# The gate stage of a PEER layer written in one fixed order, with its u products cut in pieces between the groups

## The chip, the cores and the metric

The kernel runs on one core of a Trainium2 chip. The metric is the device time of one execution in microseconds, lower is better. Engines are named as in the profile: PE (TensorE; PEld is its weight load), DVE (VectorE), ACT (ScalarE), POOL (GpSimd) and SP (SyncE, which issues DMAs).

## The reference

Two transformer blocks on 512 tokens of 1024 features: a mixer with a mixture of experts, then a second block that ends in a PEER layer. The change lies in that last layer alone. Per token it scores two sets of 128 keys for each of 8 heads, takes the best 16 of each, the best 16 of their sums, and mixes 8 x 16 of 16,384 experts:

```python
q = (ht @ wq).reshape(t, PEER_HEADS, 2, PEER_DK)
...
va, ia = lax.top_k(sa, PEER_TOPK)
vb, ib = lax.top_k(sb, PEER_TOPK)
cand = va[..., :, None] + vb[..., None, :]
cidx = ia[..., :, None] * PEER_NKEYS + ib[..., None, :]
top, pos = lax.top_k(cand, PEER_TOPK)
eidx = jnp.take_along_axis(cidx, pos, axis=-1)
g = jax.nn.softmax(top, axis=-1)
a = jax.nn.gelu(jnp.einsum('thkd,td->thk', u_tab[eidx], ht))
return jnp.einsum('thk,thkd->td', g * a, v_tab[eidx])
```

## The kernel before

The 512 tokens are four tiles of 128. For the first three (ND = 384) the kernel does not gather experts: it computes the product of all 16,384 rows of u with the tokens, 128 rows at a time (the 128 "u products", L1607 to L1620), multiplies by a gate that is zero for experts that a token did not choose, and multiplies by the rows of v (`peer_v`, matmuls into `pacc`). The fourth tile gathers its rows (`Gather`). Rows are split in two f16 halves: uTh (high) by ACT, uTl (the rest) by DVE, or, with early=True, ACT scales the raw row in place as well (uTr) and POOL subtracts (`peer_parts`, L1597). A u product is 8 slices of three matmuls, 128x384 each (`mm3`): two with uTh, the third with uTl. ACT then applies gelu into `pa`.

The pacc loop needs u products well ahead of their use (LAG = 34), so class `Ahead` makes the first ones in earlier stages: `load` fetches and splits a row block, `multiply` runs the matmuls, `finish` runs gelu; calling the object does all three, `load` only where no block is ready.

The layer runs in stages. `peer_scores` (L1412) goes in 19 steps over 16 half heads (N = 16): query products `pq`, scores `ps`, `top16` on DVE (five passes: max, index, replace, max, index), and, one head later, `pairs` (candidate sums `cand` and numbers `cidx`), `pick_best` (best 16 of 50 and a mask `pickm`), `pick_which` and `pick_sum` (the chosen experts, `pef`). The last head's picks for three tiles come in steps 16 to 18, on DVE. Each of steps 9 to 18 makes one early u product, loading the next one first. `late` keeps the fourth tile's candidates for the pacc loop.

The gate stage (`peer_gates`, L1548) then goes over the three tiles. Per tile: softmax of the picks (`pgate`, with an exp on ACT, whose table is not that of gelu, so each change loads one), expert numbers cut in two digits (`gab`), three transposes on PE (`gtp`), copies to f16 (`gidx`, `gsp`). Then groups of GN = 16 tokens: four one-hot passes on DVE (`gob`, `goa`, `goh`, `goa`, 128x2048 each), 32 matmuls (`gg`), four copies by ACT into `gst`, and for each second group a DMA of 2 MB to `gates` in memory. There are 8 groups a tile, 24 in all. Some groups also call `Ahead`, up to 31 products (LAG - REST). The stage has no manual schedule here: the recording layer's scheduler sets the order of its instructions on each engine. Three products more (`rest`) and the pacc loop follow, in manual schedule.

Of the kernel before, what the change touches and what calls it, by code (L numbers as in the profile page):

```python
# [10 lines left out]
F32 = mybir.dt.float32  # L11
F16 = mybir.dt.float16
# [7 lines left out]
P = 128  # L20
# [3 lines left out]
D = 1024  # L24
# [11 lines left out]
GC = 32  # L36
GN = 16
GS = 10
LAG = 34
# [15 lines left out]
class Block:  # L55
# [1257 lines left out]
    def peer(self):  # L1313
# [5 lines left out]
        with ExitStack() as es:  # L1319
# [92 lines left out]
    def peer_scores(self, qp, vp, hl, top, ef, late, ahead):  # L1412
# [25 lines left out]
        with tc.manual_schedule(engines={ET.Pool, ET.PE, ET.DVE, ET.Activation}):  # L1438
# [3 lines left out]
            evacuate(0)  # L1442
            for n in range(N + 3):
                h, s = divmod(n, 2)
# [21 lines left out]
                if n > 1 and s == 0 and n <= N:  # L1466
                    cand[h - 1] = self.pairs(vp, qp, [val.pop(n - 2), val.pop(n - 1)], [idx.pop(n - 2), idx.pop(n - 1)], eng)
                    for tt, m in enumerate(self.pick_best(qp, [(cand[h - 1][0][:, tt], top[:, tt, h - 1]) for tt in range(3)], eng)):
                        picks[h - 1, tt] = m

                if n > 2 and s == 1:
                    for tt in range(ND // P):
                        self.pick_which(picks[h - 1, tt], cand[h - 1][1][:, tt], n < N)
                    for j in range(2):
                        nc.scalar.activation(late[j][:, h - 1], cand[h - 1][j][:, 3], AF.Copy)
                if s == 0 or n > 8:
                    ahead.finish()
                evacuate(n + 1)
                if n < N:
                    val[n] = vp.tile([P, 4, 16], F32, name="tv", tag="tv", bufs=4)  # L1480
                    idx[n] = vp.tile([P, 4, 16], F32, name="ti", tag="ti", bufs=4)
                    for tt in range(4):
                        iu[n, tt] = qp.tile([P, 16], U32, name="tiu", tag="tiu", bufs=8)
                    self.top16(qp, [(val[n][:, tt], iu[n, tt], ps[:, P * tt:P * (tt + 1)]) for tt in range(4)], P)

    def pairs(self, vp, qp, val, idx, eng):
# [14 lines left out]

    def pick_best(self, wk, xs, eng):

        nc = self.nc
        ps = [wk.tile([P, 16], U32, name="ppos", tag="ppos", bufs=3) for _ in xs]
        self.top16(wk, [(top, pos, cand) for pos, (cand, top) in zip(ps, xs)], 50)
        ms = []
        for pos in ps:
            posf = wk.tile([P, 16], F32, name="pposf", tag="pposf", bufs=3)
            eng.tensor_copy(posf, pos)  # L1510
            m = wk.tile([P, 8 * 20 + 8 * 50], F32, name="pickm", tag="pickm", bufs=5)
            for x, k, n in self.pick_parts(m):
# [34 lines left out]

    def peer_gates(self, wk, e, g, gd, tt, ahead):  # L1548

        nc = self.nc  # L1550
        f = wk.tile([P, 2, P], F32, name="gab", tag="gab", bufs=1)
        nc.vector.tensor_scalar(f[:, 0], e, 1.0 / 128, -63.5 / 128, op0=OP.mult, op1=OP.add)
        nc.vector.tensor_scalar(f[:, 0], f[:, 0], 1.5 * 2.0 ** 23, -1.5 * 2.0 ** 23, op0=OP.add, op1=OP.add)
        nc.vector.scalar_tensor_tensor(f[:, 1], f[:, 0], -128.0, e, op0=OP.mult, op1=OP.add)
        ps = self.ps1("gtp")
        for j, x in enumerate((f[:, 0], f[:, 1], g)):
            nc.tensor.transpose(ps[:, P * j:P * (j + 1)], x, self.ident)

        twice = lambda x: x.unsqueeze(len(x.shape)).to_broadcast([*x.shape, 2])
        idx = wk.tile([P, 2, P, 2], F16, name="gidx", tag="gidx", bufs=2)  # L1560
        gs = wk.tile([P, 2, P, 2], F16, name="gsp", tag="gsp", bufs=2)
        nc.scalar.activation(idx, twice(ps[:, :2 * P].rearrange("p (j t) -> p j t", j=2)), AF.Copy)
        gp = twice(ps[:, 2 * P:3 * P])
        nc.scalar.activation(gs[:, 0], gp, AF.Copy, scale=2.0 ** GS)
        nc.vector.scalar_tensor_tensor(gs[:, 1], gp, 2.0 ** GS, gs[:, 0], op0=OP.mult, op1=OP.subtract)
        pairs = lambda x: x.rearrange("p t (i j) -> p t i j", j=2)
        iota = pairs(self.iota128[:, None, :]).to_broadcast([P, GN, P // 2, 2])
        for c in range(P // GC):
            stage = wk.tile([P, P, GC], F32, name="gst", tag="gst", bufs=2)
            for n in range(c * GC, c * GC + GC, GN):  # L1570
                col = lambda t: t[:, n:n + GN, None, :].to_broadcast([P, GN, P // 2, 2])
                b, a, hi = (wk.tile([P, GN, P], F16, name=f"go{x}", tag=f"go{x}", bufs=2) for x in "bah")
# [4 lines left out]
                for q in range(0, GN, 4):  # L1577
                    ps = self.ps1("gg")
                    for t in range(4):
                        for j, x in enumerate((hi, a)):  # L1580
                            nc.tensor.matmul(ps[:, P * t:P * (t + 1)], b[:, q + t], x[:, q + t], start=j == 0, stop=j == 1)
                    o = n - c * GC + q
                    nc.scalar.activation(stage[:, :, o:o + 4], ps.rearrange("p (t i) -> p i t", t=4), AF.Copy, scale=2.0 ** -GS)
                if (n == c * GC or c % 2) and len(ahead.a) < LAG - REST:
                    ahead(early=False)
            nc.sync.dma_start(gd[:, tt * (P // GC) + c], stage)

# [55 lines left out]

    def top16(self, wk, xs, n):

        nc = self.nc
        ts = [wk.tile([P, P], F32, name="t16", tag="t16", bufs=6) for _ in xs]
        for val, idx, x in xs:
# [74 lines left out]
class Ahead:  # L1723
# [196 lines left out]
```

## Time and profile before

| | us |
|---|---|
| median of 3 runs | 2419.8 (2419.02 to 2428.05) |
| the profiled execution, device time | 2418.51 |
| its span, first to last instruction | 2416.8 |
| PE busy | 2258.1 (93%) |
| DVE busy | 1851.5 (77%) |
| ACT busy | 1041.8 (43%) |
| POOL busy | 577.7 (24%) |

Busy time is the time in which an engine executes; register, branch, semaphore and DMA-issuing instructions do not count. Matmuls are pipelined, so a matmul of 0.33 us follows the one before it after about half of that. The scores run from about 1220 to 1378 us, the gate stage to about 1530, the pacc loop from 1547 to the end. A row of the windows view gives the busy time of PE, PEld, DVE, ACT and POOL in this order, each with its number of instructions, and PEclk, the clock that PE was granted as a share of full speed. A row of a timeline gives start, duration, engine, line, operation, output <- inputs, and in brackets the time that the engine stood idle before it and what ended that.

### The profile page before, as it was taken

What the parts mean: (1) busy time and instruction counts of PE and PEld (TensorE: products, weight loads), DVE (VectorE), ACT (ScalarE), POOL (GpSimd) and SP (SyncE); (2) the same over time, 40 slices, a digit from 0 to 9 for tenths busy, and PEclk for the clock granted to TensorE, in tenths of its full rate; (3) what the DMA queues carried; (4) which work ended last, traced back from release to release, by engine and by line L of the source; (5) the groups of instructions that cost most, each with busy time, mean ns of one, the idle gap of its engine ahead of it and who ended that gap; (6) DMA issues with size and microseconds to landing.
All of it is one profiled execution on the core that took longest, in us unless ns stands there. A gap on an engine that the chain in (4) does not pass through costs nothing.

```text
span 2416.8 us, 36514 instructions
## 1 busy us (share of the span) xinstructions
PE 2258.1 (93%) x13669; PEld 1165.9 (48%) x13669; DVE 1851.5 (77%) x3453; ACT 1041.8 (43%) x1657; POOL 577.7 (24%) x608
## 2 busy tenths in 40 slices
PE   6998889979999999899899898899999999999999
PEld 3444444435444444356355465555555555555544
DVE  5998658666666666668489999778888888888787
ACT  4545543244333333466255655443333333333333
POOL 2124000000000000001057700035545554544320
PEclk9999989989999999899999999999999999999999
DMA  4411149969999999322242256769999999999885
GB/s 135 135 45 47 37 148 324 333 226 414 418 419 419 419 419 419 137 62 78 80 142 77 62 213 240 251 235 337 349 348 345 342 352 338 346 347 343 299 295 172
DMA packets 186323, 613.17 MB, mean 254 GB/s; under 512 B 17971, under 2 KB 71772, under 8 KB 159900
## 3 DMA queue, kind: packets, MB, share of 16 engines
q1 hardware_dynamic: 148988, 476.44, 53.3%
q0 software_dynamic: 36864, 134.23, 15.5%
q8 instruction: 108, 1.77, 0.3%
q14 instruction: 75, 0.61, 0.1%
q10 hardware_dynamic: 288, 0.11, 0.0%
HBM read 579.58 MB, written 27.28 MB: 251 GB/s over the span
## 4 chain that ended last, share of the span: by engine, by line
PE 55%; DVE 11%; DMA 6%; ACT 3%; issue 2%; POOL 0%; SPq 0%; DVEq 0%; ACTq 0%; POOLq 0%
PE pacc L1641 21%; PE pu L141 16%; DMA wx<-in_w_dram 6%; PE w L779 5%; PE pj L141 4%; PE py L826 2%; PE disp L736 2%; PE wout L141 2%; DVE goa L1574 1%; DVE goh L1575 1%; PE comb L762 1%; DVE gob L1573 1%; PE pq L141 1%; DVE wlo L122 1%; DVE hT L763 1%
## 5 line engine op out<-in xcount | busy, mean ns | idle before, releaser
L141 PE MATMUL pu<-pn,uTh 128*128 128x384 f16 x2048 | 503.2, 328 | 7.1 <-ACT pa L1615 5.1
L1641 PE MATMUL pacc<-vNh,pw 128*128 128x512 f16 x1536 | 472.3, 379 | 0.0
L1641 PEld LDWEIGHTS <-pw 128*128 128x128 f16 x2304 | 225.4, 98 | 261.6
L141 PE MATMUL pu<-pn,uTl 128*128 128x384 f16 x1024 | 335.8, 328 | 7.6 <-POOL uTl L1603 4.7
L1641 PE MATMUL pacc<-vNl,pw 128*128 128x512 f16 x768 | 291.1, 379 | 0.0
L141 PEld LDWEIGHTS <-uTh 128*128 128x128 f16 x2048 | 200.7, 98 | 147.9 <-issue 7.3
L121 ACT ACTIVATE vNh<-vNr 128x1024 f16<-128x1024 f32 x128 | 135.2, 1056 | 309.0 <-issue 276.6
L122 DVE SCALAR_TENSOR_TENSOR vNl<-vNr,vNh 128x1024 f16<-128x1024 f32 x128 | 156.8, 1225 | 124.3 <-ACT vNh L121 124.2
L141 PEld LDWEIGHTS <-whi 128*128 128x128 f16 x1744 | 159.6, 99 | 182.5 <-issue 26.2
L779 PE MATMUL w<-wx,xt 128*64 128x512 f32 x1024 | 230.1, 597 | 0.0
L1769 POOL DMA_INDIRECT row<-in_pu_dram,pe x128 | 188.7, 1474 | 173.3 <-DVE row L1791 143.6
L1769 POOL DMA_INDIRECT row<-in_pv_dram,pe x128 | 171.3, 1338 | 229.2 <-DVE gacc L1798 196.4
L122 DVE SCALAR_TENSOR_TENSOR wx<-wx,w2h 128x2048 f16<-128x2048 f32 x64 | 144.8, 2289 | 66.4 <-ACT w2h L121 66.4
L141 PE MATMUL pj<-wx,whi 128*128 128x512 f16 x624 | 189.0, 383 | 2.0 <-ACT wx L121 1.8
L1162 POOL MEMSET cvu<- 128x2 f32 x4 | 0.4, 99 | 728.8 <-PE w L779 728.8
L122 DVE SCALAR_TENSOR_TENSOR wlo<-wraw,whi 128x1024 f16<-128x1024 f32 x97 | 129.8, 1340 | 50.1 <-ACT whi L121 50.0
L1798 DVE SCALAR_TENSOR_TENSOR gacc<-row,ga,gacc 128x1024 f32<-128x1024 f32 x127 | 162.8, 1282 | 2.3
L1615 ACT ACTIVATE pa<-pu 128x384 f32<-128x384 f32 x128 | 62.3, 487 | 225.8 <-PE pu L141 225.7
L122 DVE SCALAR_TENSOR_TENSOR uTl<-uTr,uTh 128x1024 f16<-128x1024 f32 x113 | 138.2, 1223 | 25.2 <-ACT uTh L121 23.4
L1791 DVE SCALAR_TENSOR_TENSOR row<-row,htok 128x1024 f32<-128x1024 f32 x128 | 150.1, 1220 | 0.0
L121 ACT ACTIVATE w2h<-wx 128x2048 f16<-128x2048 f32 x64 | 121.2, 1909 | 54.8 <-DMA wx<-in_w_dram 54.8
L141 PEld LDWEIGHTS <-uTl 128*128 128x128 f16 x1024 | 100.7, 98 | 76.4 <-POOL uTl L1603 5.5
(449 smaller groups left out, 3888.2 us busy)
## 6 DMA issues: line engine op xcount, KB each, us to landing
wx<-in_w_dram SPq DMA_DIRECT2D x192, 1024.0 KB
uTr<-in_uT_dram SPq DMA_DIRECT2D x128, 512.0 KB
vNr<-in_vN_dram SPq DMA_DIRECT2D x128, 512.0 KB
wraw<-in_win_dram SPq DMA_DIRECT2D x57, 512.0 KB
wada<-in_wada_dram SPq DMA_DIRECT2D x48, 512.0 KB
gates<-gst SPq DMA_DIRECT2D x12, 2048.0 KB
pg<-gates SPq DMA_DIRECT2D x32, 768.0 KB
wraw<-in_wq_dram SPq DMA_DIRECT2D x16, 512.0 KB
```

Source lines behind the costliest of these rows:

```text
L121: self.nc.scalar.activation(hi, src, AF.Copy, scale=scale)
L122: self.nc.vector.scalar_tensor_tensor(lo, src, scale, hi, op0=OP.mult, op1=OP.subtract)
L141: self.nc.tensor.matmul(ps, w[a][:, ks[k], :], act[b][:, k, cols], start=first and k == only[0] and j == 0, stop=last and k == only[-1] an ...
L736: nc.tensor.matmul(out[i], ut[j][:, tt, P * k:P * (k + 1)], disp[q][:, tt], start=tt == 0 and j == 0, stop=tt == 3 and j == 1)
L762: nc.tensor.matmul(ps, y[q][j][:, P * m:P * (m + 1)], comb[q], start=j == 0, stop=j == 1)
L779: nc.tensor.matmul(ps[64 * b:64 * b + 64], xt[q][:, 4 * c + k, 64 * b:64 * b + 64], w[b][:, k], start=c == 0 and k == 0, stop=c == 1 and k ...
L826: nc.tensor.matmul(py[d][64 * b:64 * b + 64], ht[x][:, f, 64 * b:64 * b + 64], w2[d][b][v][:, f], start=f == 0 and j == 0, stop=f == 3 and ...
L1615: self.nc.scalar.activation(a, ps[:, :ND], AF.Gelu_apprx_tanh, scale=UN)
L1641: self.nc.tensor.matmul(acc[2 * t + c], w[x][:, P * t:P * (t + 1)], v[y][:, 512 * c:512 * c + 512], start=ia == 0 and j == 0, stop=ia == P ...
L1769: nc.gpsimd.indirect_dma_start(out=t, out_offset=None, in_=I[table], in_offset=bass.IndirectOffsetOnAxis(ap=self.e[:, s:s + 1], axis=0))
L1791: nc.vector.scalar_tensor_tensor(x, x, 1.0, self.ht, op0=OP.mult, op1=OP.mult, accum_out=self.a[:, s:s + 1])
L1798: nc.vector.scalar_tensor_tensor(self.acc, x, self.a[:, s:s + 1], self.acc, op0=OP.mult, op1=OP.add)
```

## The change

It has three parts. The gate stage becomes one manual schedule on PE, DVE, ACT and POOL, with the groups of all three tiles in one loop. The u products of this stage are cut in 8 pieces of three matmuls (`Ahead.steps`), of which about five stand between the matmuls of one group and the next; the next block is loaded at a product's first piece. And `peer_scores` ends after step 16: the last head's picks move into the gate stage, one tile at a time (`experts`), tile 0 ahead of the first group, tiles 1 and 2 behind the one-hots of groups 1 and 3; two early products of steps 17 and 18 go with them, and four products (`ahead(early=True)`) stand ahead of the first tile's columns. Scratch for the picks is a tile of the v rows' buffers (`room`), so three v loads stand later on SP.

```diff
+PICK = 8 * 20 + 8 * 50
...
-                    self.peer_scores(qp, vp, hl, top, ef, late, ahead)
+                    cand = self.peer_scores(qp, vp, hl, top, ef, late, ahead)
                 with tc.tile_pool(name="peerg", reuse_waits="tile", bufs=1) as gp:
-                    for tt in range(ND // P):
-                        self.peer_softmax(gp, g[:, tt], top[:, tt])
-                        self.peer_gates(gp, ef[:, tt].rearrange("p h k -> p (h k)"), g[:, tt].rearrange("p h k -> p (h k)"),
-                                        gd, tt, ahead)
+                    self.peer_gates(gp, cand, top, ef, g, gd, ahead)
...
-            for n in range(N + 3):
+            for n in range(N + 1):
...
-                    for tt, m in enumerate(self.pick_best(qp, [(cand[h - 1][0][:, tt], top[:, tt, h - 1]) for tt in range(3)], eng)):
+                    best = [(cand[h - 1][0][:, tt], top[:, tt, h - 1]) for tt in range(3)] if n < N else []
+                    for tt, m in enumerate(self.pick_best(qp, best, eng)):
                         picks[h - 1, tt] = m
...
+                if n > 2 and (s == 1 or n == N):
                     for j in range(2):
-                        nc.scalar.activation(late[j][:, h - 1], cand[h - 1][j][:, 3], AF.Copy)
+                        nc.scalar.activation(late[j][:, n // 2 - 1], cand[n // 2 - 1][j][:, 3], AF.Copy)
...
+    def peer_gates(self, wk, cand, top, ef, g, gd, ahead):
...
+        def experts(tt):
+
+            room = ahead.wk.tile([P, D], F32, name="room", tag="vNraw", bufs=3)
+            m, = self.pick_best(wk, [(cand[0][:, tt], top[:, tt, 7])], nc.vector, room)
+            self.pick_which(m, cand[1][:, tt], False)
+            self.pick_sum(m, ef[:, tt, 7])
+
+        def columns(tt):
+
+            self.peer_softmax(wk, g[:, tt], top[:, tt])
+            e, f = flat(ef[:, tt]), wk.tile([P, 2, P], F32, name="gab", tag="gab", bufs=1)
...
+            cols[tt] = idx, gs
+
+        def one_hots(n):
+            if n < groups:
...
+        def sums(n):
+            b, a, hi = hot.pop(n)
...
+            if o + GN == GC:
+                nc.sync.dma_start(gd[:, c], stage.pop(c))
+
+        with self.tc.manual_schedule(engines={ET.PE, ET.DVE, ET.Activation, ET.Pool}):
+            for n in range(4):
+                ahead(early=True)
+                if n == 0:
+                    experts(0)
+            columns(0)
+            one_hots(0)
+            left = LAG - REST - len(ahead.a)
+            steps = ahead.steps(left)
+            next(steps)
+            for n in range(groups):
+                tt, m = divmod(n, per)
+                if m == 5 and tt < 2:
+                    columns(tt + 1)
+                one_hots(n + 1)
+                if m in (0, 2) and tt < 1:
+                    experts(1 + m // 2)
+                share = lambda n: KT + KT * (left - 1) * n // (groups - 1) if n >= 0 else 0
+                for _ in range(share(n) - share(n - 1)):
+                    next(steps, None)
+                sums(n)
+            for _ in steps:
+                pass
...
+    def steps(self, n):
+
+        self.load(early=False)
+        yield
+        for i in range(n):
+            if i + 1 < n:
+                self.load(early=False)
+            u = tuple(x.rearrange("p (k m) -> p k m", m=P) for x in self.u.pop(0))
+            ps = self.blk.psum.tile([P, 512], F32, name="pu", tag="u", bufs=2)
+            for k in range(KT):
+                self.blk.mm3(ps[:, :ND], u, self.hl, slice(0, ND), only=[k], first=k == 0, last=k == KT - 1)
+                if k < KT - 1:
+                    yield
+            self.ps.append(ps)
+            self.finish()
+            yield
```

How the order moves on ACT at the end of the scores, before. The first `pa` is the gelu of the 12th u product; numbers behind names are buffers.

```order
L1615 ACTIVATE pa_13853<-pu_13757 128x384
L1601 ACTIVATE uTh_13857<-uTr_13855 128x1024
L1602 ACTIVATE uTr_13855<-uTr_13855 128x1024
L1475 ACTIVATE late0_11642<-cand_13793 128x50
L1475 ACTIVATE late1_11643<-cidx_13794 128x50
L1542 ACT_TABLE_LOAD
L1542 ACTIVATE pgate_11652<-pgate_11652 128x128
L1615 ACT_TABLE_LOAD
L1615 ACTIVATE pa_13895<-pu_13862 128x384
L1601 ACTIVATE uTh_13899<-uTr_13897 128x1024
L1542 ACT_TABLE_LOAD
```

The same place now, from the `pa` of the 13th product on (the `late0` and `late1` copies and the `pa` of the 12th stand just ahead of it).

```order
L1662 ACTIVATE pa_13853<-pu_13828 128x384
L1648 ACTIVATE uTh_13870<-uTr_13868 128x1024
L1649 ACTIVATE uTr_13868<-uTr_13868 128x1024
L1662 ACTIVATE pa_13900<-pu_13875 128x384
L1648 ACTIVATE uTh_13904<-uTr_13902 128x1024
L1649 ACTIVATE uTr_13902<-uTr_13902 128x1024
L1662 ACTIVATE pa_13934<-pu_13909 128x384
L1648 ACTIVATE uTh_13938<-uTr_13936 128x1024
L1649 ACTIVATE uTr_13936<-uTr_13936 128x1024
L1662 ACTIVATE pa_13968<-pu_13943 128x384
L1544 ACT_TABLE_LOAD
L1544 ACTIVATE pgate_11652<-pgate_11652 128x128
```

Behind the 13th product's `pa` there are now three runs of uTh, uTr, pa, and the first exp (`pgate`) has moved behind the third; a uTh now stands behind the `pa` of the product before it.

DVE at the second and third group, before: one-hots of two groups stand interleaved.

```order
L1573 TENSOR_TENSOR gob<-iota_363,gidx 128x2048
L1575 TENSOR_TENSOR goh<-goa,gsp 128x2048
L1574 TENSOR_TENSOR goa<-iota_363,gidx 128x2048
L1576 TENSOR_TENSOR goa<-goa,gsp 128x2048
L1575 TENSOR_TENSOR goh<-goa,gsp 128x2048
L122 SCALAR_TENSOR_TENSOR uTl<-uTr,uTh 128x1024
L1576 TENSOR_TENSOR goa<-goa,gsp 128x2048
L1573 TENSOR_TENSOR gob<-iota_363,gidx 128x2048
L1574 TENSOR_TENSOR goa<-iota_363,gidx 128x2048
L1573 TENSOR_TENSOR gob<-iota_363,gidx 128x2048
```

DVE behind the one-hots of the second group (n = 1), now: the last `goa` of that group, one tile's picks, a uTl, the next group's first one-hot.

```order
L1595 TENSOR_TENSOR goa<-goa,gsp 128x2048
L1696 MAX ptop<-cand 128x8
L1698 MAX_INDEX room<-ptop,cand 128x8
L1700 MATCH_REPLACE room<-ptop,cand 128x50
L1702 MAX ptop<-room 128x8
L1704 MAX_INDEX room<-ptop,room 128x8
L1512 CAST room<-room 128x16
L1515 TENSOR_TENSOR room<-iota_361,room 128x160
L1515 TENSOR_TENSOR room<-iota_361,room 128x400
L1535 SCALAR_TENSOR_TENSOR room<-room,cidx 128x160
L1535 SCALAR_TENSOR_TENSOR room<-room,cidx 128x400
L1539 TENSOR_REDUCE pef<-room 128x8 x2
```

The eleven rows of the picks of a tile have moved in between two groups; before, they stood ahead of the first.

DVE between two groups where the second tile's columns stand, now.

```order
L123 SCALAR_TENSOR_TENSOR uTl<-uTr,uTh 128x1024
L1543 TENSOR_TENSOR pgate<-ptop 128x128
L1546 TENSOR_REDUCE pgs<-pgate 128x8
L1547 RECIPROCAL pgs<-pgs 128x8
L1548 TENSOR_TENSOR pgate<-pgate,pgs 128x128
L1573 TENSOR_SCALAR gab<-pef 128x128
L1574 TENSOR_SCALAR gab<-gab 128x128
L1575 SCALAR_TENSOR_TENSOR gab<-gab,pef 128x128
L1584 SCALAR_TENSOR_TENSOR gsp<-gtp,gsp 128x256
L1592 TENSOR_TENSOR gob<-iota_363,gidx 128x2048
```

The softmax, the digits and the copy for a tile stand together between two groups, so that the next `gob` has the subtract for exp, the transposes and the f16 copies ahead of it; before, the subtracts for all three exps stood ahead of the first group.

## Rows read from the trace of the kernel before

**Rows 1.** The page, part 1: busy us (share of the span) xinstructions of each engine

```profile
PE 2258.1 (93%) x13669; PEld 1165.9 (48%) x13669; DVE 1851.5 (77%) x3453; ACT 1041.8 (43%) x1657; POOL 577.7 (24%) x608
```

**Rows 2.** Stretches by windows: us, then each engine's busy us, PEclk, DMA share, GB/s

```profile
1490.00:1528.00 38.00, 30.42 (x327) 21.75 (x326) 38.00 (x35) 20.20 (x36) 0.00 (x0) 1.00 0.57 219
...
1600.00:2400.00 800.00, 800.00 (x4222) 412.89 (x4220) 664.55 (x843) 299.73 (x412) 361.42 (x259) 1.00 0.92 327
```

**Rows 3.** Chain that ended last, 1366 to 1550: start us, us, what

```profile
1480.16 1.56 PE gg L1581 x28
...
1529.35 10.25 PE pu L141 x63
...
1542.38 5.43 PE pu L141 x22
```

**Rows 4.** Timeline of ACT, POOL, PE: start us, us, engine, line, operation [idle before <-releaser]

```profile
1369.73 1.04 ACT L1601 ACTIVATE uTh<-uTr 128x1024 f16<-128x1024 f32 x1
...
1370.80 1.06 ACT L1602 ACTIVATE uTr<-uTr 128x1024 f32<-128x1024 f32 x1
...
1371.94 2.16 POOL L1603 TENSOR_TENSOR uTl<-uTr,uTh 128x1024 f16<-128x1024 f32 x1 [0.99 <-ACT uTr L1602]
...
1374.15 0.34 PE L141 MATMUL pu<-pn,uTl 128*128 128x384 f16 x1 [2.83 <-POOL uTl L1603]
...
1376.70 0.52 PE L141 MATMUL pu<-pn,uTl 128*128 128x384 f16 x1
...
1379.25 0.33 PE L141 MATMUL pu<-pn,uTl 128*128 128x384 f16 x1
```

**Rows 5.** Timeline of ACT, 1383 to 1391 and near 1540

```profile
1383.61 1.28 ACT L1542 ACT_TABLE_LOAD   x1
1384.91 0.31 ACT L1542 ACTIVATE pgate<-pgate 128x128 f32<-128x128 f32 x1
...
1389.94 0.60 ACT L1562 ACTIVATE gidx<-gtp 128x512 f16<-128x512 f32 x1 [1.98 <-PE gtp L1557]
1390.44 0.38 ACT L1564 ACTIVATE gsp<-gtp 128x256 f16<-128x256 f32 x1
...
1539.62 0.49 ACT L1615 ACTIVATE pa<-pu 128x384 f32<-128x384 f32 x1 [3.41 <-PE pu L141]
```

**Rows 6.** Timeline of DVE, 1388 to 1392

```profile
1388.88 0.28 DVE L1554 SCALAR_TENSOR_TENSOR gab<-gab,pef 128x128 f32<-128x128 f32 x1
1389.08 0.28 DVE L1544 TENSOR_REDUCE pgs<-pgate 128x8 f32<-128x128 f32 x1
...
1390.57 1.23 DVE L1573 TENSOR_TENSOR gob<-iota,gidx 128x2048 f16<-128x2048 f16 x1
1391.71 0.42 DVE L1565 SCALAR_TENSOR_TENSOR gsp<-gtp,gsp 128x256 f16<-128x256 f32 x1
```

**Rows 7.** DVE 1390 to 1530 by form (busy, mean ns, idle before), then its timeline

```profile
L122 DVE SCALAR_TENSOR_TENSOR uTl<-uTr,uTh 128x1024 f16<-128x1024 f32 x18 | 21.9, 1217 | 5.9 <-ACT uTh L121 4.3 <-PE pu L141 1.6
...
1428.38 1.22 DVE L1576 TENSOR_TENSOR goa<-goa,gsp 128x2048 f16<-128x2048 f16 x1
...
1431.79 1.22 DVE L1575 TENSOR_TENSOR goh<-goa,gsp 128x2048 f16<-128x2048 f16 x1
```

**Rows 8.** Timeline of DVE and PE at the stage's end

```profile
1526.34 1.21 DVE L1576 TENSOR_TENSOR goa<-goa,gsp 128x2048 f16<-128x2048 f16 x1
...
1547.64 0.38 PE L1641 MATMUL pacc<-vNh,pw 128*128 128x512 f16 x1
```

**Rows 9.** Timeline of DVE near 1549; then tile pickm: ns min/median/max, first, last

```profile
1548.95 0.21 DVE L1649 MAX8 late<-late 128x8 f32<-128x50 f32 x1
...
1550.01 0.20 DVE L1657 FIND_INDEX8 ppos<-late,t 128x8 uint32<-128x50 f32 x1
...
L1513 DVE TENSOR_TENSOR pickm<-iota,pposf x6: 309/435/561, 1380.4 to 1382.7; 128x160 f32<-128x160 f32 x3, 128x400 f32<-128x400 f32 x3
L1533 DVE SCALAR_TENSOR_TENSOR pickm<-pickm,cidx x6: 309/435/561, 1383.2 to 1384.8; 128x160 f32<-128x160 f32 x3, 128x400 f32<-128x400 f32 x3
```

More of the change, by code (lines that the diff above doesn't have):

```diff
@@ L1484, in peer_scores @@
                     self.top16(qp, [(val[n][:, tt], iu[n, tt], ps[:, P * tt:P * (tt + 1)]) for tt in range(4)], P)
+        return cand[N // 2 - 1]
     def pairs(self, vp, qp, val, idx, eng):
@@ L1566, in peer_gates @@
+        ET = mybir.EngineType
+        twice = lambda x: x.unsqueeze(len(x.shape)).to_broadcast([*x.shape, 2])
         pairs = lambda x: x.rearrange("p t (i j) -> p t i j", j=2)
         iota = pairs(self.iota128[:, None, :]).to_broadcast([P, GN, P // 2, 2])
[L1568 to L1572, printed above, removed]
+        flat = lambda x: x.rearrange("p h k -> p (h k)")
@@ new lines, in peer_gates @@
+        per, groups = P // GN, ND // GN
+        cols, hot, stage = {}, {}, {}
+        def experts(tt):
[6 more added lines that the diff above has]
+            e, f = flat(ef[:, tt]), wk.tile([P, 2, P], F32, name="gab", tag="gab", bufs=1)
+            nc.vector.tensor_scalar(f[:, 0], e, 1.0 / 128, -63.5 / 128, op0=OP.mult, op1=OP.add)
+            nc.vector.tensor_scalar(f[:, 0], f[:, 0], 1.5 * 2.0 ** 23, -1.5 * 2.0 ** 23, op0=OP.add, op1=OP.add)
+            nc.vector.scalar_tensor_tensor(f[:, 1], f[:, 0], -128.0, e, op0=OP.mult, op1=OP.add)
+            ps = self.ps1("gtp")
+            for j, x in enumerate((f[:, 0], f[:, 1], flat(g[:, tt]))):
+                nc.tensor.transpose(ps[:, P * j:P * (j + 1)], x, self.ident)
+            idx = wk.tile([P, 2, P, 2], F16, name="gidx", tag="gidx", bufs=2)
+            gs = wk.tile([P, 2, P, 2], F16, name="gsp", tag="gsp", bufs=2)
+            nc.scalar.activation(idx, twice(ps[:, :2 * P].rearrange("p (j t) -> p j t", j=2)), AF.Copy)
+            gp = twice(ps[:, 2 * P:3 * P])
+            nc.scalar.activation(gs[:, 0], gp, AF.Copy, scale=2.0 ** GS)
+            nc.vector.scalar_tensor_tensor(gs[:, 1], gp, 2.0 ** GS, gs[:, 0], op0=OP.mult, op1=OP.subtract)
+            cols[tt] = idx, gs
@@ L1573, in peer_gates @@
+        def one_hots(n):
+            if n < groups:
+                (idx, gs), t0 = cols[n // per], GN * (n % per)
+                col = lambda t: t[:, t0:t0 + GN, None, :].to_broadcast([P, GN, P // 2, 2])
+                b, a, hi = hot[n] = [wk.tile([P, GN, P], F16, name=f"go{x}", tag=f"go{x}", bufs=2) for x in "bah"]
                 nc.vector.tensor_tensor(pairs(b), iota, col(idx[:, 1]), op=OP.is_equal)
@@ L1576, in peer_gates @@
                 nc.vector.tensor_tensor(pairs(a), pairs(a), col(gs[:, 1]), op=OP.mult)
[L1577 to L1583, printed above, removed]
@@ L1584, in peer_gates @@
-                if (n == c * GC or c % 2) and len(ahead.a) < LAG - REST:
-                    ahead(early=False)
-            nc.sync.dma_start(gd[:, tt * (P // GC) + c], stage)
+        def sums(n):
+            b, a, hi = hot.pop(n)
+            c, o = divmod(GN * n, GC)
+            if o == 0:
+                stage[c] = wk.tile([P, P, GC], F32, name="gst", tag="gst", bufs=2)
+            for q in range(0, GN, 4):
+                ps = self.ps1("gg")
+                for t in range(4):
+                    for j, x in enumerate((hi, a)):
+                        nc.tensor.matmul(ps[:, P * t:P * (t + 1)], b[:, q + t], x[:, q + t], start=j == 0, stop=j == 1)
+                nc.scalar.activation(stage[c][:, :, o + q:o + q + 4], ps.rearrange("p (t i) -> p i t", t=4), AF.Copy, scale=2.0 ** -GS)
+            if o + GN == GC:
+                nc.sync.dma_start(gd[:, c], stage.pop(c))
@@ L1642, in peer_v, with top16 @@
                                       start=ia == 0 and j == 0, stop=ia == P - 1 and j == 2)
-    def top16(self, wk, xs, n):
+    def top16(self, wk, xs, n, room=None):
         nc = self.nc
-        ts = [wk.tile([P, P], F32, name="t16", tag="t16", bufs=6) for _ in xs]
+        ts = [wk.tile([P, P], F32, name="t16", tag="t16", bufs=6) if room is None else room[:, PICK:PICK + P] for _ in xs]
         for val, idx, x in xs:
```

27 lines of the change are left out of this document (7 added, 20 removed).

## The prediction

> **What bounds the kernel now.** I read the page's totals first: TensorE (PE) is busy 93% of the span and VectorE (DVE) 77% [rows 1]. Such shares average over stages, so I went on to the busy times by stretch [rows 2]. From 1600 to 2400 us PE is busy 800.00 of 800 us; there only an earlier start helps. The changed place is the gate stage ahead of it, and there the order is reversed: from 1490 to 1528 DVE is busy 38.00 of 38 us, PE 30.42. So in this stage the reader should count DVE's queue, and ask what keeps DVE waiting before and inside it. The first one-hot starts at 1390.57 [rows 6]; the last starts at 1526.34 and ends 1.14 later, at 1527.48; the first pacc product starts at 1547.64 [rows 8]. What moves that last start moves the end one for one. All sums are against the profiled execution, 2418.5 us (span 2416.8); the median of the runs shown, 2419.8, lies 1.3 above it.
>
> **Part 1: four early products, and the exp behind them.** This is the largest term. In the changed order ScalarE (ACT) has, after pa of the 13th u product, three times uTh, uTr, pa (products 14 to 16), and only then the table load and the exp of pgate for the first tile. Nothing of product 15 is prepared before product 14 is done: its uTh stands behind pa of 14 on ACT, and that pa waits for PE, as the one at 1539.62 does for 3.41 us [rows 5]. So the three products run one after the other, each with this cycle:
> pa 0.49 [rows 5]; uTh to uTr 1.07, uTr to GpSimd's uTl 1.14 (1369.73, 1370.80, 1371.94); uTl to the third matmul 2.21 (1374.15) [rows 4]; 4.9 in all. The two matmuls that need uTh alone are done by then. The other 22 take 22 x 0.163 = 3.6 us at full rate (63 took 10.25), but behind a wait of some microseconds they take longer: 22 took 5.43 [rows 3]. The same number took as long from 1374.15 to 1379.25 + 0.33, behind a wait of 2.83 us; there a matmul shows 0.52 instead of 0.33 [rows 4], the clock being granted at 1.2 and not 2.4 GHz. The wait will be about 4.5 us each time, so I take 5.43 each time. Cycle: 4.91 + 5.43 = 10.35; 8.5 at full rate, about 12 at the low clock throughout.
> Product 13 ends as before, at 1379.6, since nothing ahead of it on PE moves. Then pa of 16 starts at 1379.6 + 3 x 10.35 = 1410.6. Behind it: pa 0.49, table load to exp 1.30 (1383.61 to 1384.91), exp 0.31 [rows 5]; DVE's six small steps 1.49 (1389.08 to 1390.57 [rows 6]); transposes 0.78 (1388.88 + 0.28 to 1389.94), ACT's gidx 0.50 and gsp 0.38, DVE's gsp 0.42 [rows 5, 6]. Together 5.7: the first one-hot starts at 1416.3, **25.7 us later** than 1390.57. DVE has nothing else to do: it ends one tile's picks by about 1382 and then waits some 30 us. Bounds: 20 with every product at full rate, 31 at the low clock throughout.
> The Trainium skill (page ScalarE: Activation LUTs, section What ACT_TABLE_LOAD costs) gives about 1283 ns for a load and some 1380 ns of drain behind it. The first agrees with the row's 1.28; the second does not, as exp starts 1.30 us after the load's start. By the page each of the three exps would come 1.38 us later, and the sum below would be 2455.
>
> **Part 2: DVE's queue from the first to the last one-hot.** Before, it takes 136.9 us (1390.57 to 1527.48). After:
> - one-hots: 24 groups of 4, start to start 1.137 (three steps from 1428.38 to 1431.79 [rows 7]): 109.2;
> - uTl halves: 16 (17 before) at the same pace: 18.2;
> - the last head's picks for tiles 1 and 2, which stood ahead of the groups. The best 16 of 50, one tile at a time, take 1.26 (1548.95 to 1550.01 + 0.20); two pairs of passes 0.87 each (435 ns mean [rows 9]), and the sums about as much: 3.9, less the overlap of neighbours, 3.8 a tile, 7.6;
> - columns of tiles 1 and 2, each between two groups: DVE's own steps 0.28 (a subtract of the size of 1388.88) + 1.49 + 0.42 = 2.2, and waits of 0.31 for exp and 0.78 + 0.50 + 0.38 for transposes, gidx and gsp: 4.2; up to 1.3 more where the table load comes late. I take 4.5, for two 9.0; bounds 4.4 (no wait) and 11.
> Sum 144.0, **7.1 us more**; bounds 2 and 10. The picks are no new work, but the earlier time in which DVE did them is now spent waiting.
> PE in a group: 15 u matmuls x 0.163 and 32 gate matmuls (28 took 1.56), 2.4 + 1.8 = 4.2 us [rows 3], against DVE's 144.0 / 24 = 6.0. So cutting the products in pieces neither costs nor gains: PE has 1.8 us to spare in a group whatever the order. What the fixed order removes are DVE's waits among the groups, 4.3 for uTh and 1.6 for PE [rows 7]; they are in the 136.9, and the waits for columns take their place.
>
> **Edits at nothing.** Three vN loads no longer precede the scores; they stand behind the first two gate writes on SP's queue, over 100 us before the pacc loop needs them. Behind the last group both orders have 87 u matmuls, then pacc, with the write of the last gates and the read of pg beside them, so the 20.2 us from 1527.48 to 1547.64 stay. GpSimd's 16th uTl is in part 1.
>
> **Sum.** 25.7 + 7.1 = 32.8; 2418.5 + 32.8 = 2451.3, rounded to 2451.
>
> **Rivals.** *A, the early products hide (not slower).* If exp did not wait for the three products, DVE would go on: picks of tile 0 by 1382, exp by 1382.5, the first one-hot at about 1386, 4.6 earlier than now; with 7.1 more in the queue behind it 2421, and with the columns' waits hidden too 2416. It decides if ACT reaches exp by about 1390. For it: GpSimd and ACT are far from busy here, so a queue that let uTh of 15 pass would hide most. Against it: the order, in which exp stands behind pa of 16, and the wait at 1539.62, behind which ACT does nothing else [rows 5]. A gain of over 12 us has no place in it: DVE's waits among the groups are 5.9 us in all [rows 7].
> *B, the pieces cost PE its clock.* With 4.2 us of work in 6.0, PE pauses in every group. If the clock fell once in a group as behind the waits of part 1 (5.43 - 3.6 = 1.8 us lost), PE would need 6.0 of 6.0 and hardly anything would show. If it stayed low through 8 of 24 groups, PE would need 8.4 in each, 2.4 x 8 = 19 us more: 2470. Against it: from 1490 to 1528 PE is busy only 80%, with a pause in every group, and the granted clock is 1.00 [rows 2]. The Trainium skill (page Perfetto Trace Analysis, section Matmul Optimizations) wants matmuls issued back to back in batches, since the engine's power is scaled by its use; by that rule B is what pieces bring.
>
> **How the numbers follow.** Forecast 0.78: 2451, its own range by the bounds of both parts 2418.5 + 22 = 2441 to 2418.5 + 41 = 2460. A 0.11 (2416 to 2421). B 0.06 (near 2470). The other 0.05 is a partial hiding, one of the three cycles or two, near 2433. The range 2433 to 2462 leaves out A and B. This kernel's measurement can tell 0.5%, 12 us, from no change: slower 0.88 (forecast, B, most of the partial hiding), same 0.10, faster 0.02, both from A.
>
> **What would show it.** Right: three waits on PE of 4 to 5 us for GpSimd's uTl, 8 to 11 us apart; DVE idle for some 30 us before pgs, released by exp; the first one-hot near 1416, the last ending near 1560; DVE about 95% busy between them; PE full from the pacc loop on. Wrong: exp before 1395 (A); PE busier than DVE in the groups, at a low clock (B); a stage clearly shorter than 140 us, which would mean that DVE's queue was not its bound.

## The result and the profile after

| | time, median | range of runs | ratio to before |
|---|---|---|---|
| before | 2419.4 us | 2417.8 to 2428.1 | |
| changed | 2452.7 us | 2449.4 to 2457.2 | 1.0144 [1.0123, 1.0165] |
| changed, once more, beside the experiments | 2453.8 us (before: 2415.9) | 2452.6 to 2459.1 | 1.0154 [1.0134, 1.0174] |

The changed kernel is slower by 33 to 38 us in the medians. The profiled execution took 2449.4 us (span 2447.7). The page's totals differ from [rows 1] by almost nothing; the work is the same, and it ends later. Page, part 1, of the changed kernel:

```profile
PE 2260.2 (92%) x13669; PEld 1166.9 (48%) x13669; DVE 1853.6 (76%) x3452; ACT 1043.7 (43%) x1658; POOL 581.9 (24%) x609
```

To compare stages between executions a common mark is needed, since the same code ahead of the changed place took different times: the first pq matmul (the scores' first product) started at 1202.5 in this profile, at 1209.5 in that of before and between 1206.9 and 1213.7 in those of the experiments. So the table in the next section counts from that matmul. From it to the first pacc product the kernel before took 338.1 us, the changed one 376.4 and, once more, 376.1: **38 us longer**; from there to the end both take 869 to 870. The times in the rows below therefore lie 7.0 us early against those of before.

**The front.** ACT's timeline of the changed kernel (start us, us, operation, in brackets the idle time before and its releaser) answers to [rows 5]:

```profile
1372.89 0.49 ACT L1662 ACTIVATE pa<-pu 128x384 f32<-128x384 f32 x1 [2.54 <-PE pu L142]
1373.27 1.05 ACT L1648 ACTIVATE uTh<-uTr 128x1024 f16<-128x1024 f32 x1
1374.35 1.06 ACT L1649 ACTIVATE uTr<-uTr 128x1024 f32<-128x1024 f32 x1
1383.79 0.49 ACT L1662 ACTIVATE pa<-pu 128x384 f32<-128x384 f32 x1 [8.38 <-PE pu L142]
...
1394.09 0.49 ACT L1662 ACTIVATE pa<-pu 128x384 f32<-128x384 f32 x1 [7.77 <-PE pu L142]
...
1404.38 0.49 ACT L1662 ACTIVATE pa<-pu 128x384 f32<-128x384 f32 x1 [7.77 <-PE pu L142]
1404.89 1.28 ACT L1544 ACT_TABLE_LOAD   x1
1406.19 0.31 ACT L1544 ACTIVATE pgate<-pgate 128x128 f32<-128x128 f32 x1
```

The reader is to see three waits of about 8 us for PE, one behind the other, and the exp only behind the third. PE in turn waits in each cycle for GpSimd's half, which cannot be asked for earlier because its uTh stands behind the pa. PE's timeline, which answers to [rows 4]; the last two rows are the end of product 16 and the first tile's transposes:

```profile
1377.71 0.50 PE L142 MATMUL pu<-pn,uTl 128*128 128x384 f16 x1 [2.84 <-POOL uTl L1650]
...
1388.62 0.34 PE L142 MATMUL pu<-pn,uTl 128*128 128x384 f16 x1 [2.84 <-POOL uTl L1650]
...
1398.92 0.34 PE L142 MATMUL pu<-pn,uTl 128*128 128x384 f16 x1 [2.84 <-POOL uTl L1650]
...
1404.02 0.33 PE L142 MATMUL pu<-pn,uTl 128*128 128x384 f16 x1
1407.83 0.66 PE L1578 MATMUL gtp<-ident,gab 128*128 128x128 f32 x2 [3.48 <-DVE gab L1574]
```

DVE, which answers to [rows 6, 7], has nothing to do from 1373 to 1406.5, then makes the first one-hots at 1409.88, and the last pass starts at 1557.52, where before had 1526.34 [rows 8]. DVE's timeline:

```profile
1372.84 0.28 DVE L1543 TENSOR_TENSOR pgate<-ptop 128x128 f32<-128x128 f32 x1
1406.53 0.29 DVE L1546 TENSOR_REDUCE pgs<-pgate 128x8 f32<-128x128 f32 x1 [33.41 <-ACT pgate L1544]
...
1409.88 1.22 DVE L1592 TENSOR_TENSOR gob<-iota,gidx 128x2048 f16<-128x2048 f16 x1
1411.01 1.22 DVE L1593 TENSOR_TENSOR goa<-iota,gidx 128x2048 f16<-128x2048 f16 x1
1412.26 1.22 DVE L1594 TENSOR_TENSOR goh<-goa,gsp 128x2048 f16<-128x2048 f16 x1
1413.52 1.22 DVE L1595 TENSOR_TENSOR goa<-goa,gsp 128x2048 f16<-128x2048 f16 x1
1414.66 1.22 DVE L123 SCALAR_TENSOR_TENSOR uTl<-uTr,uTh 128x1024 f16<-128x1024 f32 x1
...
1420.59 0.21 DVE L1696 MAX8 ptop<-cand 128x8 f32<-128x50 f32 x1
...
1424.24 1.21 DVE L123 SCALAR_TENSOR_TENSOR uTl<-uTr,uTh 128x1024 f16<-128x1024 f32 x1
...
1451.58 0.28 DVE L1543 TENSOR_TENSOR pgate<-ptop 128x128 f32<-128x128 f32 x1
...
1455.84 1.22 DVE L1592 TENSOR_TENSOR gob<-iota,gidx 128x2048 f16<-128x2048 f16 x1
...
1557.52 1.23 DVE L1595 TENSOR_TENSOR goa<-goa,gsp 128x2048 f16<-128x2048 f16 x1
```

Three prices stand in these rows. A tile's picks between two groups take 3.65 us (1420.59 to 1424.24), a tile's columns 4.26 (1451.58 to 1455.84). And the four passes of a group start 1.13, 1.25 and 1.26 us apart, the next thing 1.14 behind the last: 4.78 us a group. The two longer steps are those between neighbours that depend on each other: `goh` reads the `goa` that the pass right before it wrote, and the last `goa` overwrites what `goh` has just read. In before, passes that stand next to one another start 1.137 apart [rows 7]: there the scheduler had put a half of a u product, a pass of the neighbouring group or a small step between any two that depend on each other.

The stretches, which answer to [rows 2] (us, busy us of PE, PEld, DVE, ACT, POOL, then PEclk, DMA share, GB/s):

```profile
1490.00:1528.00 38.00, 29.71 (x287) 21.68 (x285) 35.35 (x38) 22.44 (x39) 0.00 (x0) 0.91 0.59 222
1600.00:2400.00 800.00, 800.00 (x4245) 415.13 (x4244) 664.94 (x877) 300.30 (x413) 368.91 (x271) 1.00 0.92 328
1410.00:1470.00 60.00, 43.34 (x391) 30.05 (x392) 56.88 (x79) 30.17 (x50) 0.00 (x0) 0.80 0.50 185
1410.00:1560.00 150.00, 116.75 (x1134) 83.32 (x1135) 143.07 (x159) 79.63 (x136) 0.00 (x0) 0.90 0.60 221
```

DVE is busy 95% of the groups, PE 78%. PE's granted clock in the first 60 us of the groups is only 0.80, but no wait of DVE in the groups is for PE, so the low clock costs the stage nothing that shows here.

### The profile page after: what moved, and what is told of

Same layout as the page of the kernel before. It is cut to its first block, busy times and chain, and to the rows that moved or that the text cites. A ratio compares the mean times of both kernels' runs of the same rounds, so it can differ in the third digit from the quotient of the medians.

```text
span 2447.7 us, 36514 instructions
## 1 busy us (share of the span) xinstructions
PE 2260.2 (92%) x13669; PEld 1166.9 (48%) x13669; DVE 1853.6 (76%) x3452; ACT 1043.7 (43%) x1658; POOL 581.9 (24%) x609
## 5 line engine op out<-in xcount | busy, mean ns | idle before, releaser
L142 PE MATMUL pu<-pn,uTh 128*128 128x384 f16 x2048 | 510.1, 332 | 8.3 <-ACT uTh L1648 4.8
```

Of the source, the lines that this page charges most:

```text
L142: self.nc.tensor.matmul(ps, w[a][:, ks[k], :], act[b][:, k, cols], start=first and k == only[0] and j == 0, stop=last and k == only[-1] an ...
```

## The experiments

Stage times of every kernel, in us, from its own profile. "Front" is from the first pq matmul to the first one-hot pass; "groups" from there to the end of the last pass (its start plus 1.2); "tail" from there to the first pacc product.

| kernel | front | groups | tail | first pq to first pacc | median time | ratio to before |
|---|---|---|---|---|---|---|
| before | 181.1 | 136.9 | 20.1 | 338.1 | 2415 to 2419 | |
| changed | 207.4 | 148.8 | 20.2 | 376.4 | 2452.7 | 1.0144 |
| changed, once more | 207.1 | 148.8 | 20.2 | 376.1 | 2453.8 | 1.0154 [1.0134, 1.0174] |
| one early product | 174.2 | 152.3 | 21.7 | 348.2 | 2427.1 | 1.0040 [1.0026, 1.0055] |
| passes spread | 209.2 | 143.9 | 21.4 | 374.5 | 2457.7 | 1.0165 [1.0148, 1.0182] |
| whole products | 207.1 | 148.8 | 26.2 | 382.1 | 2459.7 | 1.0167 [1.0150, 1.0184] |
| picks ahead | 207.3 | 144.0 | 18.6 | 369.9 | 2450.6 | 1.0129 [1.0112, 1.0146] |
| one early product, passes spread | 175.9 | 146.7 | 22.2 | 344.8 | 2423.4 | 1.0026 [1.0015, 1.0036] |
| the same, uTl on GpSimd | 175.8 | 161.4 | 23.9 | 361.1 | 2443.5 | 1.0122 [1.0097, 1.0148] |
| early products prefetched | 189.4 | 149.0 | 20.3 | 358.7 | 2437.7 | 1.0083 [1.0054, 1.0112] |
| all repairs | 174.3 | 146.2 | 21.0 | 341.5 | 2420.2 | 1.0013 [0.9999, 1.0026] |

The theory was that of the prediction with one addition from the profile: the exp waits behind three serial products; DVE's queue bounds the groups; and a pass that depends on the one just before it starts 0.12 us late. The rivals were that the exp is not what holds the front, that the pieces cost PE its clock, and that the work ahead had changed too.

**The changed kernel once more.** 

> The changed kernel once more, unedited, as the common measure for the runs beside it and for the share that the work ahead of the changed place has in a run's time: in its first profile the first pq matmul started at 1202.5, in those of before and of four experiments between 1209.5 and 1213.7, on the same code. Theory (that difference is of the chip's clock on that day and no effect of the change): here too the first pq starts between 1202 and 1214, and from there to the first pacc matmul it takes 376.4 us as in the first profile, within 2; the time is 2449 to 2460. Rival (the change itself makes the work ahead of it faster): the first pq again near 1202.5 and the time near 2450.

The first pq stood at 1211.4, the time from it to pacc was 376.1, the median 2453.8. So the early start in the first profile was not the change's doing; the change costs 38 us, of which the first profile shows 31 only because the unchanged work ahead of it had taken 7 less. The granted clock over the first 600 us was 0.96 in that profile and 0.94 in this one, which goes with the theory's cause, but no run isolates it.

**One early product instead of four.**

```
-            for n in range(4):
-                ahead(early=True)
-                if n == 0:
-                    experts(0)
+            ahead(early=True)
+            experts(0)
             columns(0)
             one_hots(0)
```

> The changed kernel, but with one early u product instead of four: the exp of the first tile and the first one-hots come right behind the 13th product, and products 14 to 16 go, in pieces, between the groups (18 instead of 15 there, three uTl halves more on DVE). Theory (the exp waits in ACT's queue behind three products that run one after the other): DVE's wait for exp falls from 33.4 us to about 2; from the pa of the 13th product to the first one-hot 5.5 us instead of 37.0, so 31.5 less; DVE's queue of the groups 148.8 + 3 x 1.137 = 152.2. Time 2452.7 - 31.5 + 3.4 = about 2425 (2420 to 2430). Rival 1 (the exp is not what holds the first one-hot): 2453. Rival 2 (TensorE, whose granted clock is 0.75 to 0.85 in the first groups, becomes the bound with 18 products among the groups): the one-hots show waits for PE of 10 us or more in all and the time is 2435 or more.

ACT's timeline there: the exp follows the 13th pa at once, and now waits for DVE.

```profile
1380.59 0.49 ACT L1660 ACTIVATE pa<-pu 128x384 f32<-128x384 f32 x1 [0.76 <-PE pu L142]
1381.10 1.28 ACT L1544 ACT_TABLE_LOAD   x1
1382.64 0.31 ACT L1544 ACTIVATE pgate<-pgate 128x128 f32<-128x128 f32 x1 [0.26 <-DVE pgate L1543]
```

DVE's longest wait for exp is 0.4 us. The front is 33 us shorter, the groups 3.5 longer (3.4 expected for three more uTl halves), the tail 1.5 longer; 2427 where about 2425 was expected. The three products ahead of the first tile's columns are the cause of the front's loss, and PE takes three more products among the groups without becoming the bound. But the edit takes them out of two queues at once: in the changed kernel the tile's transposes stand behind the same products on PE. There product 16 ends at 1404.35 and the transposes start at 1407.83, so an exp moved forward on ACT alone could have brought about 3.5 us (an estimate from these two rows; no run tests it).

**Early products prefetched.** Four early products remain, and the exp stays behind the 16th.

```
             for n in range(4):
-                ahead(early=True)
+                if n < 3:
+                    ahead.load()
+                ahead.multiply()
+                ahead.finish()
```

> The changed kernel, with its four early products, but each product's uTh, uTr and uTl are asked for ahead of the product before it instead of behind its pa. The exp stays behind the pa of the 16th. Theory (the three cycles of 10.3 to 10.9 us are long because nothing of the next product is made before the last one ends): a cycle falls to 4 to 5.5 us (24 matmuls are 3.9 at full rate; two buffers for uTh let the halves of product n + 2 start when product n ends, 4.4 us), the first one-hot comes 15 to 18 us earlier, 20 to 22 us behind the 13th pa instead of 37, DVE's wait for exp about 17 instead of 33; time about 2436 (2432 to 2441). Rival (the product itself, at the low clock, takes 10 us whatever its operands do): cycles stay at 8 us or more and the time above 2445.

ACT's timeline there, the pa of products 13 to 16:

```profile
1377.67 0.48 ACT L1665 ACTIVATE pa<-pu 128x384 f32<-128x384 f32 x1
...
1384.04 0.49 ACT L1665 ACTIVATE pa<-pu 128x384 f32<-128x384 f32 x1 [3.85 <-PE pu L142]
...
1387.94 0.49 ACT L1665 ACTIVATE pa<-pu 128x384 f32<-128x384 f32 x1 [1.38 <-PE pu L142]
...
1392.66 0.49 ACT L1665 ACTIVATE pa<-pu 128x384 f32<-128x384 f32 x1 [4.23 <-PE pu L142]
```

Cycles of 6.4, 3.9 and 4.7 us instead of 10.9, 10.3 and 10.3: the front is 17.7 to 18 shorter, DVE's wait for exp 12.0 instead of 33.4. A product by itself takes 3.9 us; the rest of a cycle was the chain from pa through ACT and GpSimd back to PE.

**Passes spread.** The compare for a of group n + 1 stands between the two products of group n (three buffers for a, one of them in the v rows' space, so the picks of all tiles share one scratch tile).

```
...
-                nc.vector.tensor_tensor(pairs(b), iota, col(idx[:, 1]), op=OP.is_equal)
-                nc.vector.tensor_tensor(pairs(a), iota, col(idx[:, 0]), op=OP.is_equal)
-                nc.vector.tensor_tensor(pairs(hi), pairs(a), col(gs[:, 0]), op=OP.mult)
-                nc.vector.tensor_tensor(pairs(a), pairs(a), col(gs[:, 1]), op=OP.mult)
...
+                nc.vector.tensor_tensor(pairs(b), iota, col(idx[:, 1], n), op=OP.is_equal)
+                nc.vector.tensor_tensor(pairs(hi), pairs(a), col(gs[:, 0], n), op=OP.mult)
+                first(n + 1)
+                nc.vector.tensor_tensor(pairs(a), pairs(a), col(gs[:, 1], n), op=OP.mult)
...
```

> The changed kernel, with DVE's four passes of a group in another order, so that none reads or overwrites what the pass right before it wrote or read: the first compare for a of group n + 1 stands between the two products of group n, and a has three buffers. The same 96 passes. Theory (a pass that depends on the one just before it starts 1.25 us behind it and not 1.137): the group's four passes take 4 x 1.137 = 4.55 instead of 4.78, 24 x 0.235 = 5.6 us less; from the first to the end of the last one-hot 143.2 instead of 148.8; time about 2447. Rival (the passes are slower for another reason, such as ACT and PE reading the same tiles, or the last tile's transfers): still 4.78 a group and 2453. The front is unchanged: 37 us from the 13th pa to the first one-hot.

DVE's timeline there:

```profile
1458.56 1.22 DVE L1605 TENSOR_TENSOR gob<-iota,gidx 128x2048 f16<-128x2048 f16 x1
1459.70 1.21 DVE L1606 TENSOR_TENSOR goh<-goa,gsp 128x2048 f16<-128x2048 f16 x1
1460.83 1.22 DVE L1597 TENSOR_TENSOR goa<-iota,gidx 128x2048 f16<-128x2048 f16 x1
1461.97 1.21 DVE L1608 TENSOR_TENSOR goa<-goa,gsp 128x2048 f16<-128x2048 f16 x1
1463.10 1.22 DVE L123 SCALAR_TENSOR_TENSOR uTl<-uTr,uTh 128x1024 f16<-128x1024 f32 x1
```

Four passes take 4.54 us, and the groups 143.9: the mechanism is as expected. The time is not: 2457.7 instead of 2447. From the first pq to pacc only 1.6 to 1.9 of the 4.9 us are left. In this profile the 13th product took 4.0 us between two pa's instead of 2.9 to 3.0 ahead of the changed place, and behind the last group's sums the u products up to the end of PE's next wait take 13.06 us, where the changed kernel has 11.92, which lengthens the tail by 1.2. A gain of that size cannot be told from none in these medians. Between the two kernels with one early product the same edit takes the groups from 152.3 to 146.7, as expected, and pq to pacc from 348.2 to 344.8; the medians go from 2427.1 to 2423.4, but their ratios to before, 1.0040 and 1.0026, have intervals that overlap. So the price of dependent passes is shown in the groups and not in the whole time.

**Whole products.** `KT * (left - 1) * n // (groups - 1)` became `KT * ((left - 1) * n // (groups - 1))`, so that a group is followed by 24 matmuls or by none.

> The changed kernel, with the u products between the groups not cut: each group is followed by a whole product of 24 matmuls or by none (15 products on 24 groups, the first as before behind the first one-hots). Theory (DVE's queue is the bound among the groups, PE has 1 to 2 us to spare in a group): from the first to the end of the last one-hot 148.8 within 2 us, the time within 3 us of 2452.7. Rival (the pieces cost PE its clock, 0.75 to 0.85 granted in the first groups, and whole products would keep it): the granted clock among the groups goes back to 1.00 and the stage is shorter by 5 us or more. Third possibility: whole products make DVE wait for PE's release of the one-hot buffers, 24 x 0.163 + 1.8 = 5.7 us of PE work in a group of 4.8 to 5.9: up to 5 us longer.

The groups take 148.8, to the tenth, and the granted clock in their first 60 us is 0.83, where the pieces have 0.80: the pieces cost neither DVE's time nor PE's clock. The time, 2459.7, misses the expected 2452.7 within 3: 6.0 us come behind the groups. PE's timeline there:

```profile
1567.20 0.50 PE L142 MATMUL pu<-pn,uTl 128*128 128x384 f16 x1 [2.97 <-DVE uTl L123]
...
1572.46 0.22 PE L1606 MATMUL gg<-goh,gob 128*128 128x128 f16 x1
```

A whole product now stands ahead of the last group's sums, and its uTl behind the last passes on DVE. The last sums start at 1572.46, 6.5 us behind the end of the last pass; with pieces they start right behind it and end 1.9 behind it. The pieces are worth 6 us at this one place.

**Picks ahead.** The last head's picks of all three tiles before the first group.

```
                 if n == 0:
-                    experts(0)
+                    for tt in range(3):
+                        experts(tt)
...
-                if m in (0, 2) and tt < 1:
-                    experts(1 + m // 2)
```

> The changed kernel, with the last head's picks of all three tiles of tokens ahead of the first group, in the time in which DVE waits for exp; nothing of them is left between the groups. Theory (3.65 us a tile between groups are on DVE's path, and DVE waits 33.4 us ahead of the first group): the wait shrinks to about 26, the first one-hot stays, the groups take 148.8 - 7.3 = 141.5, and the time is 2452.7 - 7.3 = about 2445. Rival (the groups have slack, so that picks between them are hidden): 2453, and as many us of new waits on DVE.

DVE's waits among the groups (us in total, times, longest):

```profile
DVE gsp L1584 <- ACT gsp L1583: 4.8, 3, 1.7
DVE gob L1592 <- PE gg L1606: 2.2, 2, 1.6
```

The groups are 4.8 us shorter, not 7.3, since 2.2 come back as waits for PE to release a one-hot buffer: with the picks gone, PE at its lowered clock in the first groups is next. The tail is 1.6 shorter as well, since in this profile the u matmuls behind PE's last wait took 3.58 us instead of 5.17; the edit does not explain that. So 6.2 to 6.5 are saved on the way to pacc; the median is 2 to 3 lower, less than expected and hardly more than the measurement can tell.

**One early product, passes spread.** 

> Both edits together: one early u product instead of four, so that exp comes right behind the 13th product, and DVE's passes in the order in which none depends on the one just before it. Theory (the two costs are separate and add up): the first one-hot 174 us behind the first pq, the stage from the first to the end of the last one-hot 152.3 - 5.6 = 146.7, time 2427.1 - 5.5 = about 2421.5 (2418 to 2425), still not under the kernel before. Rival (with DVE faster, PE with 18 products and the one-hot sums is the bound, 113 us at full rate, more at a lower clock): the stage stays above 150, with waits on DVE for PE.

The two costs are separate: groups of 146.7 as expected, 344.8 from pq to pacc, 2423.4. DVE's waits among the groups are those for columns, 4.8 us for gsp and 0.8 for exp.

**The same, with uTl on GpSimd.** Among the groups `self.load(early=False)` became `self.load(early=True)`.

> As the combined kernel (one early product, passes spread), and the lower halves uTl of the 18 products between the groups are made by GpSimd, which does nothing there, instead of DVE (ACT makes a second, scaled copy for each, 1.06 us). Theory (DVE's queue is the bound of the stage and GpSimd works beside it): 18 x 1.137 = 20.5 us less on DVE, the stage about 126 us; PE needs 24 x 1.8 + 18 x 3.9 = 113 at full rate, so it can just follow: time about 2401 to 2410, below the kernel before. Rival 1 (DVE's passes slow down while GpSimd works, 18 x 2.13 = 38 us): the mean of a pass rises above 1.3 us, the time is 2415 to 2440. Rival 2 (PE or ACT becomes the bound): DVE waits for PE's release of one-hot buffers, the stage 135 or more, the time above 2410.

The groups are 14.7 us longer, not 20.5 shorter. GpSimd's timeline, and DVE's a little later:

```profile
1402.97 9.73 POOL L1662 TENSOR_TENSOR uTl<-uTr,uTh 128x1024 f16<-128x1024 f32 x1 [3.64 <-ACT uTr L1661]
1414.89 11.38 POOL L1662 TENSOR_TENSOR uTl<-uTr,uTh 128x1024 f16<-128x1024 f32 x1 [2.19 <-PE gg L1620]
...
1438.20 2.92 POOL L1662 TENSOR_TENSOR uTl<-uTr,uTh 128x1024 f16<-128x1024 f32 x1 [2.43 <-ACT uTr L1661]
```

```profile
1436.78 1.21 DVE L1606 TENSOR_TENSOR goh<-goa,gsp 128x2048 f16<-128x2048 f16 x1
1437.92 1.21 DVE L1597 TENSOR_TENSOR goa<-iota,gidx 128x2048 f16<-128x2048 f16 x1
1439.05 3.15 DVE L1608 TENSOR_TENSOR goa<-goa,gsp 128x2048 f16<-128x2048 f16 x1
```

Beside passes of DVE without a gap, two of the subtractions, which take GpSimd 2.12 us alone, take 9.73 and 11.38. Twelve others take 2.1 to 3.0, while a pass of DVE that meets a running one takes up to 3.15 instead of 1.22. Which of the two engines waits, and why, these rows do not settle. The 96 passes took 139.8 us in all, instead of 116.8 without the edit, so the 20.5 us taken off DVE came back as 23.0 of longer passes, and DVE waits 10.3 us for PE to release one-hot buffers (no such wait without the edit), while PE waits for the late halves (7.7 us once). The Trainium skill (SBUF — State Buffer, section Who interferes with whom) states that a DVE instruction with two SBUF inputs contends with a GpSimd instruction that reads SBUF, over ports that the two share. The passes and the subtraction are of these kinds, and the rows agree that they contend.

**All repairs.** One early product, exp ahead of its pa, passes spread, and each tile's columns in three parts:

```
...
-                if m == 5 and tt < 2:
-                    columns(tt + 1)
-                one_hots(n + 1)
+                if m in (3, 4) and tt < 2:
+                    columns(tt + 1, m - 3)
+                one_hots(n + 1, (lambda: columns(tt + 1, 2)) if m == 4 and tt < 2 else lambda: None)
```

> All that the runs so far point to: one early u product, with the exp ahead even of its pa on ACT; DVE's passes spread; and the columns of tiles 1 and 2 in three parts (subtract and exp ahead of one group; sums, columns and transposes ahead of the next; DVE's gsp between that group's passes), so that DVE waits for neither exp nor transposes. Theory (DVE's queue is the bound from the last head's picks on): against the combination of the first two, 144.8 us less 0.4 + 1.7 a tile, 4.1 in all, in the stage (about 142.6) and up to 1.7 ahead of the first one-hot (174 behind the first pq), the last part unchanged at 22: from the first pq to the first pacc 338 to 340 us, where the kernel before has 338.1: the same time as before, 2414 to 2420, and about 36 less than the changed kernel. Rival (ACT or PE becomes the bound as DVE's waits go, with 18 products at a lowered clock among the groups): the stage stays at 145 or more, with waits on DVE for PE or for uTh, and the time at 2422 or more.

The median is 2420.2, at 1.0013 [0.9999, 1.0026] of before: no difference that can be told. The waits for columns are gone but for the first tile, and DVE waits for PE instead:

```profile
DVE gob L1616 <- PE gg L1632: 4.1, 2, 2.5
DVE gsp L1596 <- ACT gsp L1592: 1.4, 1, 1.4
```

So the groups end at 146.2 and not at 142.6: theory and rival each hold for a part. No order of the fixed kind that was tried beats the kernel before.

## Why the prediction was right, and where its sum was short

- **Part 1 (25.7 us) held**: 26.0 to 26.3. Of its cycle, pa to third matmul took 4.82 us (4.91 predicted), the cycles 10.9, 10.3 and 10.3 (10.35), from the last pa to the first one-hot 5.5 (5.7). In the first cycle the matmuls behind the wait show 0.50 us from the first one on, where the other two cycles start with 0.34; so it took 10.9. Taking 5.43 for 22 matmuls, from the row behind a wait of the same kind, was the right choice between 3.6 and twice that: they took 6.05, 5.43 and 5.43. The waits of 4 to 5 us for uTl that it named as a sign came as two, 1.53 for uTh and 2.84 for uTl. One early product and the prefetch show the two halves of the mechanism: the products ahead of the first tile's columns, and the chain from product to product. The part names exp in ACT's queue alone; that the transposes stand behind the same products on PE it does not say, and its sum does not depend on it.
- **Part 2 (7.1 us) was too small**: 11.9. Picks (3.65 a tile for 3.8) and columns (4.26 for 4.5) were priced well, together 0.8 too high. The step that failed is "one-hots: 24 groups of 4, start to start 1.137". That pitch was read from passes that another pass or a uTl half kept apart; the changed order puts `goh` and the last `goa` of a group each behind a pass that it depends on, and a group takes 4.78 instead of 4.55, which is 24 x 0.235 = 5.6 us. With that, 7.1 - 0.8 + 5.6 = 11.9. The bound of 10 for this part did not hold either: no row of before showed two dependent passes side by side, and so their price should have been put in the bounds as unknown.
- **Edits at nothing held**: the tail is 20.2 (20.1). That the pieces neither cost nor gain held for DVE's queue; against whole products in the same fixed order they save 6 us at the end, which the prediction did not see, but the tail that it took from before came out right.
- **The sum** was 32.8 where the trace shows 38. That the forecast of 2451 came so near to the first median, 2452.7, is luck: in the profiled one of those runs the unchanged work ahead took 7 us less, and for the others it is not known. Against the kernel before on the same chip the repeated measurement gives 2453.8 - 2415.9 = 37.9.
- **Rival A** fell: exp started at 1406.19, not by 1390. Its price was wrong too, by the rows of PE above: even with exp early, the transposes behind product 16 would have held the first one-hot. **Rival B** had the clock right and the price wrong: granted 0.80 over the first 60 us of groups, and the one-hot sums still wait for DVE (7.4 us for goa, 3.9 for goh). The Trainium skill (page Perfetto Trace Analysis, section Matmul Optimizations) wants matmuls back to back in batches, since the engine's power is scaled by its use. Whole products, which are longer batches, had 0.83 in the same stretch, so the pieces are hardly what lowered it. Nor is it the front with its waits: with the early products prefetched, PE had 0.97 in the 40 us ahead of the first one-hot and 0.79 in the 60 us behind it. What lowered the clock stays open.
- **The table load**: the exp starts 1.30 us behind the load's start, as before, and the drain that the Trainium skill states (page ScalarE: Activation LUTs, section What ACT_TABLE_LOAD costs) does not show in the changed kernel either; the sum of 2455 by that page comes near the result for a reason that the trace does not have.

## What to carry to other kernels

When a free order is replaced by a written one, go down each in-order queue and ask, for the first instruction that another engine waits for, what now stands ahead of it; here a small exp on ACT, and the transposes that follow it on PE, stood behind three products, and that cost 26 us. A pitch read from a trace is the pitch of its neighbours: where the new order sets dependent operations side by side, the price of the pair is unknown, and belongs in the range. And moving work to an engine that lies idle helps only if that engine does not slow the one it is to relieve: here 20.5 us taken off DVE came back as 23.0.

## What the runs showed of the hardware

- Two DVE passes (128 x 2048, f16) of 1.22 us start 1.137 us apart when the second does not depend on the first, and 1.25 to 1.26 apart when it reads what the first wrote or overwrites what the first read; with one other pass between them the price is gone (four passes take 4.54 us instead of 4.78).
- GpSimd's 2.12 us subtraction took up to 11.38 us beside DVE's unbroken passes, and a pass of 1.22 up to 3.15 us beside it.
- With the same code ahead of the changed place, the first pq matmul started anywhere from 1202.5 to 1213.7 us. A stage is better measured from a mark of its own than from the start of the span.
